# A hybrid encoder layer on one core: the gates' first weight loads, the turning of the keys, and four pins on VectorE's order

## The chip, the core and the metric

The kernel runs on one core of a Trainium2 chip. Five instruction streams work side by side: TensorE (PE, with its weight loads shown apart as PEld), VectorE (DVE), ScalarE (ACT), GpSimd (POOL) and SyncE (SP), which in this kernel only issues transfers. Each stream takes its instructions in the order in which the program lists them, so one that has to wait also holds up those behind it on its engine. Transfers are issued by SP and POOL (a few at the start by ACT) and carried by 16 DMA engines. The metric is the device time of one execution in microseconds; the time before is 641.28 us, the median of three runs (641.11 to 642.57).

## What is computed

One transformer-like layer on x of 512 tokens by 2048 features, all in float32:

```
h    = rms_norm(x, norm_w)
proj = h @ w_in                      # 2048 x 4608
q, k, v, g_attn, xr, g_lru = split(proj)
attn = softmax(rope(rms(q)) @ rope(rms(k)).T / sqrt(128)) @ v     # 8 heads, 2 key/value heads
lru  = scan_fwd(conv(xr)) + scan_bwd(conv(xr))                    # gated linear recurrence
mixed = [rms_norm(attn) * silu(g_attn), rms_norm(lru) * silu(g_lru)]
out  = x + mixed @ w_out             # 2048 x 2048
```

Every operand is held as a high part (a cast to fp32r) and a low part (the rest after subtracting the high part), and each product is three matmuls: high by high, high by low, low by high (`mm3`, lines 151 to 154).

## The kernel before

**Weights.** A weight chunk is 256 rows by 512 columns (512 KB). `wload` (line 219) issues its load on SP into one of three slots of a ring (`wring`), ACT casts its two halves to `wh` (line 216), and DVE subtracts them to `wl` (line 217), which frees the ring slot. A projection of 512 columns takes eight chunks; in each chunk PE runs 24 matmuls of 128x512, four steps of six. Loads and splits are given a priority 600 instructions ahead of their place in the text.

**Who sets the order.** PE's order is written out by hand. The order on ACT, DVE, POOL and (outside the attention) SP is chosen by a scheduler from priorities and its own estimate of when operands are ready; it is fixed when the program is built. `tc.issue_after(ins)` adds an edge of order: what the block issues on the engine of `ins` comes behind `ins` there. It adds no wait between engines. Inside the attention, SP's order is that of the text.

**The stages.** Nine projections of 512 columns follow each other on PE: two for the recurrence's input, one for keys and values, two for the queries (four heads each), then four for the gates, of which three run as `gates()` under the attention and one after it; the output projection ends the kernel. A generator `fill` yields after each of the four steps of a chunk, and `weave(fill, chain)` runs it in turn with a chain of other work: the chain yields the number of steps of `fill` to run before it goes on.

During the two query projections (64 steps) the chain is `kv` (line 581): the keys' norm and rotation, then the turning of the keys. To turn a pair of heads, `sent` (line 548) runs four DVE transposes per pair and writes the result aside to DRAM (SP, 512 KB); `landed` (line 565) reads it back with four SP transfers of 128 KB into a tile `lq`, of which there are two; `split_head` (line 575) makes the high part on ACT and the low part on DVE. The two pairs of queries from the first query projection are sent aside after its 32 steps and read back by two calls of `next_pair` (line 680). `kv` also splits the values, sums the squares of the recurrence's output (`lru_squares`), and at its end forms the factor `gbc` of the group norm.

**Gates and attention.** Before the attention, three chunks of gate weights are fetched ahead. The attention goes by units: unit `i` is head `i // 4` and block `i % 4` of 128 queries. It starts after `BEGIN` = 11 steps of the gates. `weights` (line 617) does three score matmuls into `sc`, the row maximum on DVE (`mx`, line 627), the exponential on ACT (`p`, line 629), the normalisation on POOL and a transpose on DVE (`u`, line 632). Each two units, `moved` (line 637) writes the transposed weights aside (`pd`), reads them back (`pt`), and splits them into high `ph` (ACT) and low `pl` (DVE), both on line 651; `ph` and `pl` have one buffer each, and a head has two halves. `values` (line 654) multiplies them with the values, ten units after the head's first. Two steps of the gates run between units.

A finished gate projection is evacuated by `evac_bc` (line 386): four DVE products, one for each of its four PSUM banks. This happens at units 10 and 26, which are also the units in which `values` of heads 0 and 4 are issued.

Of the kernel before, what the change touches and what calls it, by code (L numbers as in the profile page):

```python
# [21 lines left out]
NT = SEQ // P  # L22
HD = 128
NH = 8
NKV = 2
# [37 lines left out]
def hybrid_kernel(  # L63
# [20 lines left out]
    nc = tc.nc  # L84
# [63 lines left out]
    def f(ap):  # L148
        return ap.bitcast(F32)
# [42 lines left out]
    def v1(r):  # L192
        return vec[:, r : r + 1]
# [80 lines left out]
    rbc = const([P, SEQ], "rbc")  # L274
# [76 lines left out]
    def drain(fill):  # L351
        for _ in fill:
            pass
# [29 lines left out]
    hp, ap_ = [None] * (NB // 2), [None] * (NH // 2)  # L383
    sums = {}

    def evac_bc(acc):

        res = []
        with tc.high_priority():
            for a in acc:  # L390
                e = ev()
                nc.vector.tensor_mul(e, a, rbc)
                res.append(e)
        return res

# [82 lines left out]
    def lru_squares():  # L478

        hsum = pools["rot"].tile([P, 2, SEQ], F32, tag="hsum", name="hsum")  # L480
        nc.scalar.activation(hsum, hp[0], AF.Square)
        for pair in hp[1:]:
            yield 2
            sq = pools["rot"].tile([P, 2, SEQ], F32, tag="hsq", bufs=1, name=nm("hsq"))
            nc.scalar.activation(sq, pair, AF.Square)
            nc.vector.tensor_add(hsum, hsum, sq)
        sums["l"] = hsum[:, 0, :]
        nc.gpsimd.tensor_add(sums["l"], sums["l"], hsum[:, 1, :])
# [54 lines left out]
    vh = [None] * NT  # L543
    vl = [None] * NT

    asides, last_landed = [], [None]

    def sent(es, nh, *us):

        us = us or [  # L550
            pools["rot"].tile([P, NQ, 2, NT, B], F32, tag="uq", bufs=2, name=nm("uq"))
            for _ in range(nh // 2)
        ]
        for n, u in enumerate(us):
            for t, e in enumerate(es):
                nc.vector.transpose(
                    u[:, :, :, t, :].rearrange("p b h r -> p h b r"),
                    e[:, 2 * n : 2 * n + 2].rearrange("p h (b c) -> p h b c", c=B),
                )
            aside_ = dram.tile([P, NQ, 2 * SEQ // NQ], F32, name=nm("qd"), tag="qd", bufs=5)  # L560
            yield
            nc.sync.dma_start(aside_, u.rearrange("p b h t r -> p b (h t r)"))
            asides.append(aside_)

    def landed(aside_):

        to = pools["qkv"].tile([P, NQ, 2, NT, B], F32, tag="lq", bufs=2, name=nm("lq"))
        src = aside_.rearrange("(i c) b x -> b c i x", c=B)
        for b in range(NQ):
            last_landed[0] = nc.sync.dma_start(  # L570
                to[b * B : (b + 1) * B].rearrange("p i h t r -> p i (h t r)"), src[b]
            ).ins
        return to

    def split_head(pair, k, hi, lo):
# [3 lines left out]
        nc.vector.tensor_sub(lo, src, f(hi))  # L579

    def kv(es):
        drain(sent(norm_rope(es, NKV, rk), NKV))
        pair = landed(asides.pop(0))
        yield 20
        opened("wx", "right")
        for t in range(NT):
            vv = es[t][:, NKV * HD :]
            vt = aside(
                lambda *a: pools["qkv"].tile(*a, tag="v", bufs=NT, name=nm("v")), 2 * NKV * HD // H
            )  # L590
            vh[t], vl[t] = vt[:, 0, :], vt[:, 1, :]
            nc.scalar.copy(vh[t], vv)
            nc.vector.tensor_sub(vl[t], vv, f(vh[t]))
        yield from lru_squares()
        for h in range(NKV):
            yield (16, 4)[h]
            kt = pools["qkv"].tile([P, 2, SEQ], F32R, tag="kt", bufs=NKV, name=nm("kt"))
            kth[h], ktl[h] = kt[:, 0, :], kt[:, 1, :]
            split_head(pair, h, kth[h], ktl[h])
        r = group_rstd(sums["l"], "r_l", NB * P)  # L600
        yield 4
        rows(
            gbc, r,
            lambda: pools["rope"].tile([P, NT, P], F32R, tag="kv", bufs=NT, name=nm("kv")),
        )
# [6 lines left out]
        qs[h] = q[:, 0, :], q[:, 1, :]  # L612
        split_head(pairs[h // 2], h % 2, *qs[h])

    pts = {}

    def weights(q, g, t, turned_, first=()):

# [18 lines left out]
    def moved(turned_, half, his):  # L637

        aside_ = dram.tile([P, NQ, NT * H // NQ], F32, name=nm("pd"), tag="pd", bufs=2 * NH)
        nc.sync.dma_start(aside_, turned_.rearrange("p a s t c -> p a (s t c)"))  # L640
        yield
        if half == 0:
            his += [at(n, 1, (NT, 2, NQ, H // NQ), F32R) for n in ("ph", "pl")]
        pt = at("pt", 2, (NQ, NT, H // NQ))
        src = aside_.rearrange("(i r) a x -> a r i x", r=B)
        for a in range(NQ):
            nc.sync.dma_start(
                pt[a * B : (a + 1) * B].rearrange("p i s x -> p i (s x)"), src[a]
            )
        hi, lo = (v[:, :, half].rearrange("p s i x -> p i s x") for v in his[:2])  # L650
        his[2:] = [nc.scalar.copy(hi, pt).ins, nc.vector.tensor_sub(lo, pt, f(hi)).ins]  # L651
        yield

    def values(h, hi, lo):
# [25 lines left out]
    def next_pair():  # L680
        pairs.append(landed(asides.pop(0)))

    def attention():

        with tc.high_priority(AHEAD):
            for h in range(2):
                turned(h)
        yield BEGIN
        writes = []
        last, units = NH * NT, {}  # L690
        for i in range(last + NT + LATE):
            h, t = divmod(i, NT)
            if i < last:
                if t % 2 == 0:
                    u = at("u", 4, (NQ, NT, 2, B))
                first = pts[h - 2][2:] if h > 1 and t == 1 else ()
                weights(qs[h], h // G, t, u, first)
                if t == 0 and 0 < h < NH - 1:
                    turned(h + 1)
                if t % 2:  # L700
                    units[i] = moved(u, t // 2, pts.setdefault(h, []))
            for j in (i - 1, i - 3):
                if j in units:
                    next(units[j])
            if i < 2:
                es = [e[:, 2 * i : 2 * i + 2] for e in rot]
                writes.append(sent(es, 2, at("u", 4, (NQ, 2, NT, B))))
                next(writes[i])
            elif i < 4:
                drain(writes[i - 2])  # L710
            if t == 2 and h % 2 and asides:
                next_pair()
            j = i - NT - LATE
            if j >= 0 and j % NT == NT - 1:
                values(j // NT, *pts.pop(j // NT)[:2])
            yield STEPS + (last <= i < last + NT)


    def gate(gs, pairs, row, sig):

        for e, g in enumerate(gs):
            if e == 0 or sig:
                ss = [sig()] if sig else gs
                with ExitStack() as stack:
                    for parts in pts.values():
                        if parts:
                            stack.enter_context(tc.issue_after(parts[2]))
                    for s, src in zip(ss, [g] if sig else gs):
                        nc.scalar.activation(s, src, AF.Silu)
            s = ss[0] if sig else g  # L730
            yield 4
            dst = pairs[e // 2][:, e % 2, :]
            nc.vector.scalar_tensor_tensor(dst, dst, v1(row + e), s, op0=ALU.mult, op1=ALU.mult)
# [341 lines left out]
    with tc.high_priority():  # L1075
# [7 lines left out]
        first = [wsplit(raw, 0, nc.vector.tensor_copy)]  # L1083
# [4 lines left out]
    for step in proj_feat(C_XR, a1, first, given):  # L1088
# [8 lines left out]
        c, e = step  # L1097
# [30 lines left out]
    rq, rk = rope_consts()  # L1128
# [18 lines left out]
    def both():  # L1147
        yield from q_proj(C_Q, a4)
        drain(sent(rot, G))
        for _ in range(2):  # L1150
            next_pair()
        yield from q_proj(C_Q + SEQ, a5)

    fill = with_sums(both(), 3)
# [18 lines left out]
    late = []  # L1173
# [5 lines left out]
    def fetch():  # L1179
        for at_ in itertools.islice(chunks_, 1):  # L1180
            fetched.append(wload(w_in, *at_))
# [5 lines left out]
    def gates():  # L1187
        todo = iter(())
        for n, (c0, row) in enumerate(((C_GL, R_LN), (C_GL + SEQ, R_LN + 4), (C_GA, R_AN))):
            acc, wait = [], 0  # L1190
            for k, _ in enumerate(proj_feat(c0, acc, take=take)):
                if n == 0 and k >= 16 and k % 4 == 0:
                    normed(hp[k // 4 - 4])
                if wait == 0:
                    wait = next(todo, 99)
                wait -= 1
                yield
            if n < 2:
                todo = gate(evac_bc(acc), hp[2 * n : 2 * n + 2], row, None)
            else:  # L1200
                late.extend(evac_bc(acc))

    with tc.issue_after(last_landed[0]):
        for _ in range(3):
            fetch()
    fill = with_sums(gates(), 2)
    with tc.manual_schedule(engines={mybir.EngineType.SP}):
        weave(fill, attention())
# [41 lines left out]
    acc = []  # L1250
# [76 lines left out]
```

## Time and profile before

| | us |
|---|---|
| median of three runs | 641.28 |
| the profiled execution | 643.89 |
| its span, first to last instruction | 641.8 |
| PE busy | 630.6 |
| DVE busy | 492.6 |
| ACT busy | 340.7 |
| POOL busy | 102.8 |

The profiled execution is 2.6 us above the median, and 2.1 us of its time lie outside the span. PE is busy in 98% of the span; the busy time of a matmul in the profile overlaps that of the next one, so the start-to-start distance of matmuls says more than their duration. In the rows of a timeline the columns are the start, the duration, the engine, the line, the operation, what it writes and reads, its shape, and in brackets how long its engine was idle just before it and what ended that. In the view by windows each engine has its busy time and instruction count, and then follow the granted clock of TensorE, the mean busy share of the DMA engines and GB/s.

### The profile page before, as it was taken

Reading aid. Unit: us, or ns where it says so; the run is one execution under the profiler, and the core shown is the slowest. Engines: PE = TensorE matmul, PEld = TensorE weight load, DVE = VectorE, ACT = ScalarE, POOL = GpSimd, SP = SyncE. Lnnn points to the kernel's source line nnn. Section 1 sums busy time; section 2 is a strip of 40 time slices with the busy share of each in tenths; the row PEclk is TensorE's granted clock in tenths of the full one; section 3 lists DMA queues with packets and bytes.
Section 4 is the critical chain, followed back from the end, with each engine's and each line's share of the span. In section 5 each row is a group of like instructions: output and inputs, shape, how many; then the busy total and the mean of one; then the engine's idle time right before and its main releaser. Section 6 shows DMA issues by size and latency. Waiting matters only on the chain.

```text
span 641.8 us, 8300 instructions
## 1 busy us (share of the span) xinstructions
PE 630.6 (98%) x2795; PEld 517.3 (81%) x2795; DVE 492.6 (77%) x808; ACT 340.7 (53%) x582; POOL 102.8 (16%) x137
## 2 busy tenths in 40 slices
PE   9999999999999999989999999999999999999997
PEld 6888888888888788778778778888888888888885
DVE  5879688986689792777787788638979867787775
ACT  3534799479945811644484447436545544433441
POOL 0000210112002531512123211201220001010010
PEclk9999999999999999989999999999999999999999
DMA  9844585859676399369739556842996676797152
GB/s 296 286 136 134 142 199 158 180 142 199 209 230 208 103 196 248 91 173 267 214 127 270 180 176 176 241 120 65 247 241 201 200 259 216 272 358 237 66 197 99
DMA packets 71435, 124.48 MB, mean 194 GB/s; under 512 B 6376, under 2 KB 27488, under 8 KB 71392
## 3 DMA queue, kind: packets, MB, share of 16 engines
q1 hardware_dynamic: 63360, 106.11, 52.1%
q0 software_dynamic: 7712, 17.31, 14.3%
q10 hardware_dynamic: 320, 0.53, 0.3%
q8 instruction: 22, 0.36, 0.2%
q14 instruction: 21, 0.17, 0.1%
HBM read 108.72 MB, written 36.18 MB: 226 GB/s over the span
## 4 chain that ended last, share of the span: by engine, by line
PE 74%; DVE 11%; ACT 6%; DMA 4%; issue 2%; POOL 2%; SPq 0%; DVEq 0%; ACTq 0%; POOLq 0%
PE mm L948 13%; PE pj L152 13%; PE pj L153 13%; PE pj L154 13%; PE pj L948 10%; PE mm L153 3%; DVE wl L217 3%; PE mm L154 3%; PE mm L152 3%; DMA wr<-in_w_in_dram 2%; ACT wh L216 1%; ACT sh L525 1%; DVE pl L651 1%; PE mm L242 1%; DMA pt<-pd 1%
## 5 line engine op out<-in xcount | busy, mean ns | idle before, releaser
L152 PE MATMUL pj<-x,wh 128*128 128x512 f32 x376 | 148.0, 394 | 0.1
L154 PE MATMUL pj<-x,wl 128*128 128x512 f32 x376 | 147.2, 392 | 0.2 <-DVE wl L217 0.2
L153 PE MATMUL pj<-x,wh 128*128 128x512 f32 x376 | 147.2, 391 | 0.0
L216 ACT CAST wh<-wr 128x512 fp32r<-128x512 f32 x143 | 85.7, 618 | 105.6 <-PE pj L153 37.5
L217 DVE TENSOR_TENSOR wl<-wr,wh 128x512 fp32r<-128x512 f32 x144 | 99.1, 715 | 30.5 <-ACT wh L216 29.8
L800 ACT CAST wh<-wr 128x1024 fp32r<-128x1024 f32 (+1 forms) x72 | 60.7, 860 | 75.0 <-PE mm L948 37.5
L801 DVE TENSOR_TENSOR wl<-wr,wh 128x1024 fp32r<-128x1024 f32 (+1 forms) x72 | 68.7, 984 | 27.3 <-ACT wh L800 27.2
L154 PEld LDWEIGHTS pj<-x,wl 128*128 128x128 f32 x376 | 70.9, 189 | 15.6 <-DVE wl L217 0.6
L152 PEld LDWEIGHTS pj<-x,wh 128*128 128x128 f32 x376 | 70.9, 189 | 15.5 <-ACT ev L513 0.8
L153 PEld LDWEIGHTS pj<-x,wh 128*128 128x128 f32 x376 | 70.9, 189 | 14.9 <-DVE x L245 0.3
L152 PE MATMUL pj<-wh,x 128*128 128x512 f32 x192 | 75.0, 391 | 0.2 <-ACT ev L513 0.2
L154 PE MATMUL pj<-wh,x 128*128 128x512 f32 x192 | 74.7, 389 | 0.0
L153 PE MATMUL pj<-wl,x 128*128 128x512 f32 x192 | 74.7, 389 | 0.0
L824 POOL DMA_DIRECT2D t<-in_w_out_dram x40 | 33.6, 918 | 139.1 <-DMA t<-in_w_out_dram 96.7
L948 PE MATMUL mm<-wh,mh 128*128 128x512 f32 x128 | 49.8, 389 | 0.0
L948 PE MATMUL mm<-wl,mh 128*128 128x512 f32 x128 | 49.8, 389 | 0.0
L948 PE MATMUL mm<-wh,ml 128*128 128x512 f32 x128 | 49.8, 389 | 0.0
L152 PEld LDWEIGHTS pj<-wh,x 128*128 128x128 f32 x192 | 36.0, 188 | 8.3 <-ACT ev L513 0.8
L154 PEld LDWEIGHTS pj<-wh,x 128*128 128x128 f32 x192 | 36.0, 188 | 7.6
L153 PEld LDWEIGHTS pj<-wl,x 128*128 128x128 f32 x192 | 36.0, 188 | 7.3
L629 ACT ACTIVATE p<-mm,mx 128x512 f32<-128x512 f32 x32 | 21.9, 685 | 33.1 <-DVE mx L627 33.0
L631 POOL TENSOR_SCALAR p<-p,sm 128x512 f32<-128x512 f32 x32 | 23.7, 745 | 95.5 <-DVE sm L630 95.5
(203 smaller groups left out, 1050.0 us busy)
## 6 DMA issues: line engine op xcount, KB each, us to landing
wr<-in_w_in_dram SPq DMA_DIRECT2D x71, 512.0 KB, 4.2
wr<-in_w_out_dram SPq DMA_DIRECT2D x24, 512.0 KB, 5.0
t<-in_w_out_dram POOLq DMA_DIRECT2D x40, 256.0 KB, 6.9
wr<-t SPq DMA_DIRECT2D x40, 256.0 KB, 5.2
pd<-u SPq DMA_DIRECT2D x16, 512.0 KB, 3.0
pt<-pd SPq DMA_DIRECT2D x64, 128.0 KB, 3.7
t<-in_w_out_dram SPq DMA_DIRECT2D x24, 256.0 KB, 4.9
t<-t SPq DMA_DIRECT2D x16, 256.0 KB, 5.4
```

Source lines behind the costliest of these rows:

```text
L152: nc.tensor.matmul(acc, lh, rh, start=start, stop=False)
L153: nc.tensor.matmul(acc, lh, rl, start=False, stop=False)
L154: nc.tensor.matmul(acc, ll, rh, start=False, stop=stop)
L216: copy(hi, raw[:, k, :])
L217: nc.vector.tensor_sub(lo, raw[:, k, :], f(hi))
L242: nc.tensor.transpose(pt[:, t * P : (t + 1) * P], xc[:, t, ks], ident)
L629: nc.scalar.activation(p, sc, AF.Exp, bias=mx, accum_out=sm)
L631: last_pool[0] = nc.gpsimd.tensor_scalar(p, p, sm, 0.0, op0=ALU.mult, op1=ALU.add).ins
L800: nc.scalar.copy(hi[:, to], b)
L801: nc.vector.tensor_sub(lo[:, to], b, f(hi[:, to]))
L824: nc.gpsimd.dma_start(dst, src, accum_op=ALU.add)
L948: nc.tensor.matmul(dst[s], lh[:, ts_], rh, start=i == 0 and j == 0, stop=i == 7 and j == 2)
```

## The change

It has three parts.

1. The three gate chunks that are fetched ahead are no longer pinned behind the last read of the turned queries. The two calls of `next_pair`, which read the first query pairs back, move from the middle of the query projections (after the first pairs are sent) to behind these three fetches.
2. In `kv` the keys are still normed and rotated first, but their transposes and their write aside come after `lru_squares` and two more steps, the read back six steps after that, and the first split twelve steps later. The splits fall at steps 46 and 50 instead of 42 and 46; the group norm's factor follows four steps later too.
3. `moved` keeps the instructions of both halves (`his +=`), where before the second half's replaced the first's. The maximum and exponential of a head's block 0 are pinned behind the split of half 0 of the head two before, and those of block 1 behind half 1's, as before. When `values` is issued, the four split instructions of its head are kept in `summed`; the second to fourth products of a gate's evacuation are pinned behind them.

```
-    def evac_bc(acc):
+    def evac_bc(acc, first=()):
...
-            for a in acc:
+            for n, a in enumerate(acc):
                 e = ev()
-                nc.vector.tensor_mul(e, a, rbc)
+                with ExitStack() as stack:
+                    for ins in first if n else ():
+                        stack.enter_context(tc.issue_after(ins))
+                    nc.vector.tensor_mul(e, a, rbc)
...
     def kv(es):
-        drain(sent(norm_rope(es, NKV, rk), NKV))
-        pair = landed(asides.pop(0))
+        turned_k = sent(norm_rope(es, NKV, rk), NKV)
         yield 20
...
         yield from lru_squares()
+        yield 2
+        drain(turned_k)
+        yield 6
+        pair = landed(asides.pop(0))
         for h in range(NKV):
-            yield (16, 4)[h]
+            yield (12, 4)[h]
...
-        his[2:] = [nc.scalar.copy(hi, pt).ins, nc.vector.tensor_sub(lo, pt, f(hi)).ins]
+        his += [nc.scalar.copy(hi, pt).ins, nc.vector.tensor_sub(lo, pt, f(hi)).ins]
...
-                first = pts[h - 2][2:] if h > 1 and t == 1 else ()
+                first = pts[h - 2][2 + 2 * t : 4 + 2 * t] if h > 1 and t < 2 else ()
...
-                values(j // NT, *pts.pop(j // NT)[:2])
+                hi, lo, *summed[:] = pts.pop(j // NT)
+                values(j // NT, hi, lo)
...
-                            stack.enter_context(tc.issue_after(parts[2]))
+                            stack.enter_context(tc.issue_after(parts[-2]))
...
         drain(sent(rot, G))
-        for _ in range(2):
-            next_pair()
         yield from q_proj(C_Q + SEQ, a5)
...
+            evacs = evac_bc(acc, summed)
             if n < 2:
-                todo = gate(evac_bc(acc), hp[2 * n : 2 * n + 2], row, None)
+                todo = gate(evacs, hp[2 * n : 2 * n + 2], row, None)
             else:
-                late.extend(evac_bc(acc))
-
-    with tc.issue_after(last_landed[0]):
-        for _ in range(3):
-            fetch()
+                late.extend(evacs)
+
+    for _ in range(3):
+        fetch()
+    for _ in range(2):
+        next_pair()
```

The variable `last_landed` goes away with the pin. No instruction that computes is added or removed.

More of the change, by code (lines that the diff above doesn't have):

```diff
@@ L544, in hybrid_kernel @@
     vl = [None] * NT
-    asides, last_landed = [], [None]
+    asides = []
     def sent(es, nh, *us):
@@ L569, in landed @@
         for b in range(NQ):
-            last_landed[0] = nc.sync.dma_start(
+            nc.sync.dma_start(
                 to[b * B : (b + 1) * B].rearrange("p i h t r -> p i (h t r)"), src[b]
-            ).ins
+            )
         return to
@@ L613, in turned @@
         split_head(pairs[h // 2], h % 2, *qs[h])
-    pts = {}
+    pts, summed = {}, []
     def weights(q, g, t, turned_, first=()):
```

## The prediction

> **What bounds the kernel now.** I read the page's header first, then the waits of PE, then the windows in which they fall, and last the timelines of PE, DVE, ACT and SP there.
>
> ```profile
> span 641.8 us, 8300 instructions
> PE 630.6 (98%) x2795; PEld 517.3 (81%) x2795; DVE 492.6 (77%) x808; ACT 340.7 (53%) x582; POOL 102.8 (16%) x137
> ```
>
> PE bounds the kernel, and no matmul is added or taken away. So the change can win only the places where PE does not keep its pace, and lose by making new ones. The pace is in the chain of work that ended last: twelve matmuls of 128x512 in 2.72 us, 0.227 us each.
>
> ```profile
> 484.84 2.72 PE mm L948 x12
> ```
>
> The waits of PE and two windows show where it falls behind:
>
> ```profile
> PE mm L153 <- DVE pl L651: 2.8, 4, 1.0
> PE mm L154 <- DVE q L579: 2.2, 1, 2.2
> PE pj L152 <- ACT ev L513: 0.2, 1, 0.2
> PE pj L154 <- DVE wl L217: 0.2, 1, 0.2
> ...
> 271.00:280.00 9.00, 6.80 (x23) 5.15 (x22) 5.51 (x10) 3.19 (x5) 2.35 (x3) 0.81 1.01 228
> 300.00:385.00 85.00, 82.22 (x358) 66.40 (x357) 67.10 (x112) 45.74 (x86) 18.59 (x24) 1.00 0.66 196
> ```
>
> Four waits are for the low part `pl` of softmax weights, one is for the low part of a query head, and two short ones lie at the gates' beginning. In the window 271 to 280 the granted clock is 0.81. The timeline of PE gives each its true cost, the start-to-start distance less 0.227:
>
> ```profile
> 255.42 0.39 PE L154 MATMUL pj<-wh,x 128*128 128x512 f32 x1
> 255.93 0.50 PE L152 MATMUL pj<-x,wh 128*128 128x512 f32 x1
> ...
> 262.58 0.39 PE L153 MATMUL pj<-x,wh 128*128 128x512 f32 x1
> 263.15 0.50 PE L154 MATMUL pj<-x,wl 128*128 128x512 f32 x1 [0.18 <-DVE wl L217]
> ...
> 271.90 0.39 PE L153 MATMUL mm<-kt,q 128*128 128x512 f32 x1
> 274.49 0.50 PE L154 MATMUL mm<-kt,q 128*128 128x512 f32 x1 [2.20 <-DVE q L579]
> ...
> 310.51 0.39 PE L152 MATMUL mm<-ph,v 128*128 128x512 f32 x1
> 311.90 0.50 PE L153 MATMUL mm<-pl,v 128*128 128x512 f32 x1 [1.00 <-DVE pl L651]
> ```
>
> That is 0.28, 0.34, 2.36 and 1.16 us. The last shows that a wait costs 0.16 more than its bracket says, so the four waits for `pl` cost 2.8 + 4 x 0.16 = 3.4. The low clock costs (1 - 0.81) x 9 = 1.7. In all 0.28 + 0.34 + 2.36 + 1.7 + 3.4 = 8.1 us stand to be won.
>
> **Part 1, the gates' loads.** SP, then ACT, then DVE:
>
> ```profile
> 237.44 4.01 SPq L570 DMA_DIRECT2D lq<-qd  x8
> 241.69 32.53 SPq L205 DMA_DIRECT2D wr<-in_w_in_dram  x7
> ...
> 252.54 1.14 ACT L216 CAST wh<-wr 128x512 fp32r<-128x512 f32 x2 [18.33 <-DMA wr<-in_w_in_dram]
> 255.20 0.68 ACT L513 ACTIVATE ev<-pj,rstd 128x512 f32<-128x512 f32 x1
> 266.88 1.30 ACT L216 CAST wh<-wr 128x512 fp32r<-128x512 f32 x2 [1.16 <-PE pj L153]
> 268.09 1.14 ACT L578 CAST q<-lq 128x512 fp32r<-128x512 f32 x2
> ...
> 236.06 1.28 DVE L217 TENSOR_TENSOR wl<-wr,wh 128x512 fp32r<-128x512 f32 x2
> 259.55 0.69 DVE L530 TENSOR_TENSOR ev<-ev,rr 128x512 f32<-128x512 f32 x1 [3.53 <-POOL rr L271]
> 271.93 0.69 DVE L539 TENSOR_TENSOR ev<-ev,sq 128x512 f32<-128x512 f32 x1
> 272.54 1.29 DVE L217 TENSOR_TENSOR wl<-wr,wh 128x512 fp32r<-128x512 f32 x2
> 273.75 1.29 DVE L579 TENSOR_TENSOR q<-lq,q 128x512 fp32r<-128x512 f32 x2
> ```
>
> Eight reads of queries hold SP until 241.4, and only then does the first gate chunk go out. It lands at 252.5, and ACT stood 18.3 us for it. Behind that cast in ACT's order sits the first evacuation of the second query projection (255.20). Its PSUM bank was complete three steps of six matmuls before PE's last one at 255.42, at 255.42 + 0.39 - 3 x 6 x 0.227 = 251.7, so ACT is 3.5 us late. Everything behind inherits that: the squares, the reciprocal roots on POOL (which release DVE at 259.55), the rotation on DVE (to 272.6), then a gate chunk's `wl` and the query's low part at 273.75, for which PE stands from 272.1.
>
> After the change the three loads need only ring slots. The last slot comes free with the last `wl` of the query projection (236.06 + 1.28 = 237.3), the others a chunk and two chunks (5.4 us each) earlier. So the three loads can go out between about 226.5 and 237.4 instead of from 241.7 on, and the eight reads follow. Their 4.0 us of issue stay, and they land no later than the saturated transfers of the next window end:
>
> ```profile
> 237.00:253.00 16.00, 16.00 (x72) 13.22 (x71) 5.58 (x6) 0.46 (x1) 4.09 (x5) 1.00 1.05 249
> ...
> lq<-qd SPq DMA_DIRECT2D x8, 128.0 KB, 6.4
> wr<-in_w_in_dram SPq DMA_DIRECT2D x6, 512.0 KB, 11.1
> ```
>
> The DMA share is 1.05 there, so the same bytes in another order end at the same time: three loads (1.5 MB) ahead of the reads push these back by up to 1.5 MB / 249 GB/s = 6 us. A read that began at 241 and takes 6.4 lands by 254, and its first user on ACT stands at 268.09: hidden. At 11.1 us a load the first gate chunk is there by 238 and the third by 249, ACT evacuates on time, and the chain behind it moves 3.5 us forward: rotation to 269.1, `wl`, which needs ACT's casts of 266.88 (these wait for PE and do not move, done 268.2), to 270.4, and the query's low parts to 271.1 and 271.7. PE wants the first at 272.1. So the 2.36 go, with 1.0 to spare; the 0.28 go (the evacuation is what PE waited for), and the 0.34 go because the second gate chunk's last cast no longer stands behind late squares. What is late next is this same low part, and it has 1.0 us.
>
> The clock: it is low right after the 2.6 us gap and not behind the 1.4 us gap at 310.51 (1.00 in 300 to 385). I take it to go with the gap: 1.7. Part 1 is worth 0.28 + 0.34 + 2.36 + 1.7 = 4.7 us.
>
> [...]
>
> **Part 2, the keys.** Four transposes, one write of 512 KB, four reads, two casts, two subtractions and the group norm's small operations move later by one chunk of 5.4 us or (transposes, write, first reads) by about 5.
>
> ```profile
> L556 DVE STREAM_TRANSPOSE uq<-kv x4: 434/438/441, 195.8 to 202.8; 128x256 f32<-128x256 f32 x4
> L579 DVE TENSOR_TENSOR kt<-lq,kt x2: 643/664/684, 217.8 to 231.2; 128x512 fp32r<-128x512 f32 x2
> ```
>
> On DVE 4 x 0.44 = 1.8 us leave the stretch before 203 and return behind the sums of squares; nothing waits for keys until 271, so 2 x 0.66 of splits at 231 to 237 have 34 us of cover. The second split frees the tile `lq` for the second pair of queries; it then ends at about 237, when the reads are to begin: at worst they start a microsecond later, inside their cover. On SP one write and four reads move past three or four weight loads; each issue is about 0.4 us and the loads keep their priority. On POOL the group norm's two small operations, and the accumulating transfers behind them, wait up to 5.4 us longer, for sums that the output projection (first matmuls at 484.84) takes up. I take zero; the bounds are a gain of 0.1 (the last short wait of PE on an evacuation) and a loss of 1.8, the transposes if they push a `wl` that PE waits for and nothing covers them.
>
> **Part 3, the pins.** DVE around the first wait for `pl`, then around the second, with ACT:
>
> ```profile
> 308.66 0.69 DVE L392 TENSOR_TENSOR ev<-pj,rbc 128x512 f32<-128x512 f32 x1 [0.22 <-PE pj L154]
> 310.02 0.69 DVE L392 TENSOR_TENSOR ev<-pj,rbc 128x512 f32<-128x512 f32 x1 [0.67 <-PE pj L154]
> 310.63 1.22 DVE L651 TENSOR_TENSOR pl<-pt,ph 128x1024 fp32r<-128x1024 f32 x1
> ...
> 322.98 0.69 ACT L629 ACTIVATE p<-mm,mx 128x512 f32<-128x512 f32 x1 [3.21 <-DVE mx L627]
> 323.66 1.04 ACT L651 CAST ph<-pt 128x1024 fp32r<-128x1024 f32 x1
> ...
> 327.71 1.22 DVE L651 TENSOR_TENSOR pl<-pt,ph 128x1024 fp32r<-128x1024 f32 x1
> ```
>
> At 308.66 and 310.02 DVE waits for PE to finish banks of the gate, while `pl`, which PE wants at 310.7, stands behind. With the second to fourth product pinned behind it, `pl` starts by 308.5 and ends by 309.7: the 1.16 go, and again at unit 26. The pinned products lose 1.2 us; their banks are wanted four gate steps and two units later, 4 x 6 x 0.227 + 2 x 0.7 = 6.8 us, so that hides.
>
> At 322.98 ACT has stood 3.2 us for a maximum, with `ph` of half 0 behind it. The pin on block 0 puts this cast and its `pl` ahead of that exponential and maximum; half 1, whose `pl` now ends at 328.9, then follows about 2 us earlier, and its wait is only (2.8 - 2 x 1.0) / 2 + 0.16 = 0.56. The pinned maximum comes at most one `pl` (1.2) later, and its result is used several units on. The waits of heads 1 and 3 go as well, unless a read back lands late; I leave one of them. Part 3 is worth 3.4 - 0.56 = 2.8.
>
> **The sum.** 4.7 + 0 + 2.8 = 7.5 us off the profiled 643.9 gives 636.4. That execution stands 2.6 above the median, which the same gain takes from 641.3 to 633.8. From no change a measurement here can tell 0.3%, 1.9 us: faster is below 639.4.
>
> **The rivals.**
> *Only one of the two parts pays.* DVE's order is chosen anew, and the query's low part could stay behind the rotation and a gate's `wl`; or the read back, not DVE's order, makes `pl` late. For it speaks that the margin in part 1 is 1.0 us; against it, that the rows show data ready and only order in the way. 641.3 - 2.8 - 0.6 = 637.9, or 641.3 - 4.7 = 636.6. Chance 0.14.
> *The low clock stays.* [...] Against it, one dip in the whole span and that behind the longest gap. Chance 0.08.
> *The queries come too late (slower).* The eight reads now follow the loads on SP, and SP waits in order for ring slots:
>
> ```profile
> SPq L205 <- DVE wl L217: 187.3, 39, 10.4
> ```
>
> If the reads fall behind the later gate loads as well, the query's parts come behind PE. A read needs 2 us (first four issues), 6.4 to land, 0.6 to cast and 0.7 to subtract, so reads issued after 272.1 - 9.7 = 262.4 make a stall. It eats what the rest gains (0.6 + 2.8) and ends slower than 643.2 once it exceeds 2.36 + 3.4 + 1.9 = 7.7 us, with reads issued after 270. The run of seven loads ends at 241.69 + 32.53 = 274.2: behind it the stall is 11.8 us and the time 641.3 + 11.8 - 2.36 - 3.4 = 647.3. Against it, the reads stand before the fourth load in the text. Chance 0.22, other new waits of that size included.
> *The gains are given back* in new short waits, 639.4 to 643.2: chance 0.06.
>
> **How the numbers follow.** The forecast has the remaining 0.50. Faster: 0.50 + 0.14 + 0.08 = 0.72; same 0.06; slower 0.22. Its own range is 632.8 (8.1 won, and 0.4 for the spread of the runs) to 636.1 (1.8 lost in part 2, the other short wait of 0.56 in part 3). To leave out no more than 2 in 10 the range takes in the partial cases, no change, and the slower rival's cheap end: 632.5 to 644.5.
>
> **What would show it.** Right: the first load of a gate chunk ahead of the eight reads on SP; ACT's first evacuation near 251.7; the query's low part before PE's third score matmul, and the clock 1.00 there; on DVE `pl` ahead of the second product of a gate's evacuation; no wait of PE for `pl` above 0.5. Wrong: reads of queries behind a fourth gate load, a PE gap before the first scores, or a wait of PE on `wl` between 205 and 255, where it now keeps its pace.

## The result, and the profile after

The changed kernel takes 633.86 us, the median of five runs (633.61 to 634.36), against 641.28 for the kernel before (640.89 to 643.4): a ratio of 0.9877, 95% interval 0.9859 to 0.9895. The profiled execution took 634.36 against 643.89, so 9.5 us less, where the medians differ by 7.4. That difference of 2.1 us is taken up below.

Two places of the page after: its header, and the split by engine of the chain that ended last:

```profile
span 632.2 us, 8303 instructions
PE 625.8 (99%) x2795; PEld 516.4 (82%) x2795; DVE 492.9 (78%) x808; ACT 341.6 (54%) x582; POOL 104.5 (17%) x137
...
PE 98%; DMA 1%; ACT 0%; DVE 0%; ACTq 0%; DVEq 0%; issue 0%
```

The instruction counts of the engines are those of before, and so is the work of DVE and ACT to 1 us. PE alone now carries 98% of the chain. All waits of PE that are left, and then two windows, one where the scores begin and one over 80 us of the attention:

```profile
PE mm L1071 <- POOL ones L160: 1.1, 1, 1.1
PE pj L310 <- DVE wh L216: 0.6, 1, 0.6
```

```profile
267.00:276.00 9.00, 9.00 (x41) 7.26 (x40) 7.05 (x13) 4.55 (x9) 2.35 (x3) 1.00 1.02 226
296.00:376.00 80.00, 80.00 (x352) 65.80 (x351) 64.69 (x109) 45.27 (x86) 18.62 (x23) 1.00 0.69 199
```

Both waits belong to the first 10 us of the span; from there to its end no two matmuls start more than 0.34 us apart. The waits on `pl`, on `q`, on the evacuation and on `wl` are gone, PE is busy in the whole of both windows, and the clock is 1.00 in them.

**Where the 9.5 us went.** I put the matmuls of the two profiled executions side by side, in PE's order, and took the start before less the start after. The order is the same but for the group norm's small matmuls, which come a chunk later after the change (part 2). This table is worked out from some 2,800 pairs; each row is the step by which the distance grows at one place:

| place in the trace before | gained there, us | forecast, us |
|---|---|---|
| up to 211: wait on a query evacuation | 0.45 | 0 (part 2) |
| 211 to 258, most of it at the gates' start (255 to 258) | 0.67 | 0.28 |
| 263.15, `wl` of the second gate chunk | 0.5 | 0.34 |
| 274.49, low part of a query | 2.37 | 2.36 |
| the low clock behind it | 1.61 | 1.7 |
| four waits for `pl` | 1.27 + 0.65 + 0.66 + 1.27 = 3.85 | 3.4 - 0.56 = 2.8 |

**Part 1 in the trace after.** The timeline of SP, ACT, DVE and PE at the places that the forecast named:

```profile
227.14 0.39 SPq L205 DMA_DIRECT2D wr<-in_w_in_dram  x1
...
235.83 0.38 SPq L205 DMA_DIRECT2D wr<-in_w_in_dram  x1
236.27 0.93 SPq L573 DMA_DIRECT2D lq<-qd  x2
237.30 0.40 SPq L205 DMA_DIRECT2D wr<-in_w_in_dram  x1
237.74 4.67 SPq L573 DMA_DIRECT2D lq<-qd  x5
...
251.19 0.69 ACT L516 ACTIVATE ev<-pj,rstd 128x512 f32<-128x512 f32 x1 [1.42 <-PE pj L154]
...
268.54 1.29 DVE L217 TENSOR_TENSOR wl<-wr,wh 128x512 fp32r<-128x512 f32 x2
269.75 1.29 DVE L582 TENSOR_TENSOR q<-lq,q 128x512 fp32r<-128x512 f32 x2
...
270.25 0.39 PE L153 MATMUL mm<-kt,q 128*128 128x512 f32 x1
270.49 0.50 PE L154 MATMUL mm<-kt,q 128*128 128x512 f32 x1
270.82 0.39 PE L152 MATMUL pj<-x,wh 128*128 128x512 f32 x1
```

The first gate load goes out at 227.1, the other two between the reads of queries, at 235.8 and 237.3. ACT evacuates at 251.19, and what releases it is now PE, not a load. The gate chunk's `wl` stands at 268.54 and two low parts of queries from 269.75. The first of the two takes about half of the 1.29, so it ends near 270.4, and PE takes it at 270.49, 0.24 after its last matmul. That is only just in time: the matmul lasts 0.50 instead of 0.39, as the ones behind a wait do, and the next one starts 0.33 later instead of 0.227, so about 0.1 us is still lost here. In that stretch the loads have become quicker and the reads slower, as the view of the DMA issues between 225 and 270 shows (columns: size, and the median from issue to landing):

```profile
wr<-in_w_in_dram SPq DMA_DIRECT2D x7, 512.0 KB, 7.3
...
lq<-qd SPq DMA_DIRECT2D x8, 128.0 KB, 10.4
```

A gate load lands in 7.3 instead of 11.1, a read of queries in 10.4 instead of 6.4, and nothing waits for the reads.

**Part 3.** DVE around the first half of head 0, with PE behind it:

```profile
301.49 0.68 DVE L395 TENSOR_TENSOR ev<-pj,rbc 128x512 f32<-128x512 f32 x1
...
302.71 1.18 DVE L657 TENSOR_TENSOR pl<-pt,ph 128x1024 fp32r<-128x1024 f32 x1
303.82 1.27 DVE L395 TENSOR_TENSOR ev<-pj,rbc 128x512 f32<-128x512 f32 x2
...
304.86 0.39 PE L152 MATMUL mm<-ph,v 128*128 128x512 f32 x1
305.09 0.39 PE L153 MATMUL mm<-pl,v 128*128 128x512 f32 x1
```

`pl` stands behind the first product of the evacuation and ahead of the others. It ends at 303.9, and PE uses it at 305.09, one pitch after the matmul before.

### The profile page after: what moved, and what is told of

The parts are those of the page before. It is cut to its first block, busy times and chain, and to the rows that moved or that the text cites. A ratio compares the mean times of both kernels' runs of the same rounds, so it can differ in the third digit from the quotient of the medians.

```text
span 632.2 us, 8303 instructions
## 1 busy us (share of the span) xinstructions
PE 625.8 (99%) x2795; PEld 516.4 (82%) x2795; DVE 492.9 (78%) x808; ACT 341.6 (54%) x582; POOL 104.5 (17%) x137
## 4 chain that ended last, share of the span: by engine, by line
PE 98%; DMA 1%; ACT 0%; DVE 0%; ACTq 0%; DVEq 0%; issue 0%
PE pj L152 20%; PE pj L153 20%; PE pj L154 20%; PE mm L955 14%; PE pj L955 10%; PE mm L154 3%; PE mm L152 3%; PE mm L153 3%; DMA wr<-in_w_in_dram 1%; PE mm L242 1%; PE pj L310 0%; PE mm L749 0%; PE mm L290 0%; DVE cb L986 0%; ACT wh L216 0%; ACT x L244 0%
## 5 line engine op out<-in xcount | busy, mean ns | idle before, releaser
L217 DVE TENSOR_TENSOR wl<-wr,wh 128x512 fp32r<-128x512 f32 x144 | 100.4, 723 | 22.0 <-ACT wh L216 20.9
L955 PE MATMUL pj<-wl,mh 128*128 128x512 f32 x96 | 37.4, 389 | 0.0
```

What stands on the lines that cost most here:

```text
L217: nc.vector.tensor_sub(lo, raw[:, k, :], f(hi))
L955: nc.tensor.matmul(dst[s], lh[:, ts_], rh, start=i == 0 and j == 0, stop=i == 7 and j == 2)
```

## The experiments

Theory A is the prediction's own account: the three parts pay each at its place, the low clock belongs to the gap of 2.6 us, and part 2 is worth nothing. The theories set against it stand in the expectations with their numbers. Kernels of one group ran on one chip and share its runs of the kernel before, whose median was 643.1 in the first group, 643.42 in the second and 642.46 in the third; so each time is read against its own group.

### The kernel before, once more

No edit. This asks how far its executions lie apart, and whether each has the low clock.

> The kernel before, unchanged, to see how far its executions differ from each other. [...] Rival (the dip is a fixed cost): all executions have the same clock and differ by under 1 us.

642.36 (640.03 to 644.35, 12 runs) against 643.1 (639.59 to 645.84, 28 runs); ratio 0.9991, 0.9971 to 1.0012. Over all 40 executions the mean clock sorts the times:

| mean clock of the execution | executions | median us | from - to |
|---|---|---|---|
| 0.997 and below | 16 | 644.09 | 643.04 - 645.84 |
| 0.998 | 5 | 643.13 | |
| 0.999 and above | 19 | 641.79 | 639.59 - 643.25 |

In the other two groups 5 of 7 and 2 of 12 executions of the kernel before have a mean clock of 0.997 or below. The profiled execution has a gap as long as the first one's, and no low clock in it. The timeline of ACT and DVE, and then the window:

```profile
255.41 0.62 ACT L216 CAST wh<-wr 128x512 fp32r<-128x512 f32 x1 [1.58 <-DMA wr<-in_w_in_dram]
255.93 0.68 ACT L513 ACTIVATE ev<-pj,rstd 128x512 f32<-128x512 f32 x1
...
274.49 1.28 DVE L579 TENSOR_TENSOR q<-lq,q 128x512 fp32r<-128x512 f32 x2
```

```profile
271.00:280.00 9.00, 6.80 (x30) 5.30 (x30) 7.06 (x13) 3.29 (x6) 2.35 (x3) 1.00 0.99 208
```

PE is busy 6.80 us in the window, as in the execution of the prediction, but gets 30 matmuls done instead of 23: 7 x 0.227 = 1.6 us. So the gap is in both profiled executions of this kernel, and a low clock in some 4 of 10 executions of this group. The cast at 255.41 is 0.74 later than in the first profile (254.67), yet the gap is not longer: PE has already lost time at the gates' start, to the evacuation behind that cast: the distance there is 1.38 (255.29 to 256.67), where the first profile has 0.51. A later landing is thus paid in two places, at the gates' start and at the gap. The median of before contains only part of the 1.7; the profiled execution that the sum was made from has it whole.

### Part 1 alone

The kernel before, with this edit:

```
-        for _ in range(2):
-            next_pair()
         yield from q_proj(C_Q + SEQ, a5)
...
-    with tc.issue_after(last_landed[0]):
-        for _ in range(3):
-            fetch()
+    for _ in range(3):
+        fetch()
+    for _ in range(2):
+        next_pair()
```

> The kernel before with part 1 alone (the three gate fetches unpinned, the two reads of query pairs behind them). Theory A (part 1 pays by itself: the first gate chunk lands early, ACT evacuates the query projection on time, the query's low part is ready): 641.3 - 4.7 = 636.6, no PE gap before the first scores, the four waits for pl still there. Rival B (part 1 needs the keys out of its way): a gap of over 1 us stays before the first scores, 639 or more.

638.45 (638.15 to 639.05, 9 runs); ratio 0.9935, 0.9915 to 0.9954: 4.65 us off 643.1. The timeline of ACT and DVE:

```profile
251.69 0.69 ACT L513 ACTIVATE ev<-pj,rstd 128x512 f32<-128x512 f32 x1 [1.42 <-PE pj L154]
270.25 1.29 DVE L579 TENSOR_TENSOR q<-lq,q 128x512 fp32r<-128x512 f32 x2
```

PE's waits on `q` and `wl` are gone; those on `pl` stand as they were, four with 2.8 us in all. Moving the loads takes the gap away by itself, and the spread between executions with it: 0.9 us here, 6.3 for the kernel before.

### Part 2 alone, and the change without part 1

The first is the kernel before with the edit of `kv` only:

```
-        drain(sent(norm_rope(es, NKV, rk), NKV))
-        pair = landed(asides.pop(0))
+        turned_k = sent(norm_rope(es, NKV, rk), NKV)
...
+        yield 2
+        drain(turned_k)
+        yield 6
+        pair = landed(asides.pop(0))
         for h in range(NKV):
-            yield (16, 4)[h]
+            yield (12, 4)[h]
```

> The kernel before with part 2 alone (keys transposed, sent aside and read back later). Theory A: no more than 0.5 us either way, 640.8 to 641.8, the gap of 2.6 us before the first scores and the four waits for pl unchanged. Rival B (the keys' move is what frees the stage): the gap shrinks, 638 or less.

663.74 (663.04 to 664.53); ratio 1.0321, 1.0277 to 1.0365. The second is the changed kernel with the fetches pinned again and `next_pair` back in its old place:

> The changed kernel with part 1 undone (fetches pinned behind the last read, reads in their old place). Theory A: 633.9 + 4.7 = 638.6, the gap of 2.6 us before the first scores back, no wait for pl. Rival B (the keys' move did it): 635 or less.

660.49 (659.2 to 661.03); ratio 1.0264, 1.0246 to 1.0282. Both times miss every expectation, and for one reason. The list `asides` is taken from the front. With the reads of queries in their old place and the keys sent aside later, those reads come before the keys' own: the keys are read from the aside of a query pair and a query pair from that of the keys, so the output is another, and the three reads stand in another order on the two tiles `lq`. The trace of part 2 alone, first the waits of PE and of SP's queue, then SP's timeline:

```profile
PE pj L152 <- ACT wh L216: 23.5, 1, 23.5
...
SPq L570 <- DVE q L579: 30.2, 1, 30.2
```

```profile
234.43 35.08 SPq L570 DMA_DIRECT2D lq<-qd  x8
269.55 12.18 SPq L205 DMA_DIRECT2D wr<-in_w_in_dram  x5
```

The third tile waits for a buffer that the queries' splits free, 30.2 us, and the gates' loads stand behind that read on SP; PE then waits 23.5 for the first gate chunk. This doesn't measure what part 2 is worth. It shows that part 2 needs part 1's move of the reads, and what a read with no free buffer costs on a queue that works in order.

### Part 3 alone

The kernel before with all pins; the main lines of the edit are:

```
+                    for ins in first if n else ():
+                        stack.enter_context(tc.issue_after(ins))
...
-        his[2:] = [nc.scalar.copy(hi, pt).ins, ...
+        his += [nc.scalar.copy(hi, pt).ins, ...
...
-                first = pts[h - 2][2:] if h > 1 and t == 1 else ()
+                first = pts[h - 2][2 + 2 * t : 4 + 2 * t] if h > 1 and t < 2 else ()
```

> The kernel before with part 3 alone (both pins). Theory A: the gap before the first scores stays, the four waits for pl go, 641.3 - 3.4 = 637.9 (638.5 if one is left). Rival C (pl was late because the read back was late, and the pins only relabel the wait): waits for pl of 2 us or more stay in sum, 640 or more.

640.24 (635.21 to 641.59, 10 runs); ratio 0.9944, 0.9917 to 0.997: 2.9 us off, with 1.9 to 5.3 in its interval, where 3.4 was expected. All four waits for `pl` are gone. The longest wait of PE behind the start is now this one:

```profile
PE mm L154 <- DVE q L582: 0.5, 1, 0.5
```

and the timeline of ACT and DVE is:

```profile
251.74 0.62 ACT L216 CAST wh<-wr 128x512 fp32r<-128x512 f32 x1 [1.22 <-DMA wr<-in_w_in_dram]
252.26 0.69 ACT L516 ACTIVATE ev<-pj,rstd 128x512 f32<-128x512 f32 x1
270.81 1.28 DVE L582 TENSOR_TENSOR q<-lq,q 128x512 fp32r<-128x512 f32 x2
```

The wait on `q` is 0.5 here, not 2.2. This is the fastest of the ten executions, 635.21, and its third half of gate weights landed in time for a cast at 251.74, where the profiled executions of the unedited kernel had it at 254.67 and 255.41. The first evacuation follows that cast in ACT's order, and the low part of the query follows the evacuation at a nearly constant distance in all traces: 18.55 here, 18.55 and 18.56 in the two of before, 18.56 in part 1 alone, 18.56 after. So the gap's size hangs on when that load lands (and, where the load is so late that PE stands at the gates' start, on how much is paid there first), and differs from one execution to the next.

### The change without part 2

The changed kernel with `kv` as before.

> The changed kernel with part 2 undone (keys turned early again). Theory A: within 0.5 us of the changed kernel's 633.9, at most one short wait of 0.4 us back at the start of the second query projection. Rival B: the gap before the first scores comes back in part, 635 or more.

634.95 (634.51 to 635.55); ratio 0.987, 0.9852 to 0.9887 against 643.42. One wait of PE is back:

```profile
PE pj L152 <- ACT ev L516: 0.2, 1, 0.2
```

In the timeline this is a distance of 0.59 between matmuls at 209.78 and 210.37, 0.36 above the pitch, and the next one, to 210.71, is 0.11 above it. The times can't tell 0.5 us across groups, so part 2 is worth the 0.47 that this trace shows, or the 0.45 of the two profiled executions: little, but not the zero of the sum. The wait stands in all five traces without part 2 and in none of the nine with it. The rows show how it goes: the evacuation stands on ACT behind squares of the recurrence's output, which wait for a sum on DVE. Before, that sum starts at 204.62, behind the keys' transposes, and the evacuation at 209.71; after, they start at 202.43 and 208.40.

### The change without the pin on the evacuation

```
...
-                    for ins in first if n else ():
-                        stack.enter_context(tc.issue_after(ins))
```

> The changed kernel without the pin on the gates' evacuations, the pin on block 0's maxima kept. Theory A (two causes, two pins): the waits of heads 0 and 4 come back, 1.2 us each, those of heads 1 and 3 do not: 633.9 + 2.4 = 636.3. Rival D (one chain: the late evacuation is what makes head 1 late too): three waits or more, 636.8.

636.61 (636.12 to 636.75); ratio 0.9894, 0.988 to 0.9909; 1.7 above the kernel without part 2 of the same group (the changed kernel itself was not run in this group; with part 2's 0.47 taken off that kernel, the pin is worth about 2.1). PE's wait, and the timeline of DVE at the first of two places:

```profile
PE mm L153 <- DVE pl L654: 2.0, 2, 1.0
```

```profile
303.80 0.69 DVE L392 TENSOR_TENSOR ev<-pj,rbc 128x512 f32<-128x512 f32 x1 [0.67 <-PE pj L154]
304.41 1.22 DVE L654 TENSOR_TENSOR pl<-pt,ph 128x1024 fp32r<-128x1024 f32 x1
```

This is the picture of before, six us earlier: DVE waits for PE's banks with `pl` behind. The waits of heads 0 and 4 are back, each a distance of 1.39 on PE, and those of heads 1 and 3 are not. The pin does what the prediction said, for these two heads alone.

### The change without the pin on block 0

```
-                first = pts[h - 2][2 + 2 * t : 4 + 2 * t] if h > 1 and t < 2 else ()
+                first = pts[h - 2][4:6] if h > 1 and t == 1 else ()
```

> The changed kernel without the pin on block 0's maxima, the pin on the gates' evacuations kept. Theory A: the waits of heads 1 and 3 come back, 0.6 us each, 633.9 + 1.2 = 635.1. Rival D: only head 3's comes back, 634.5, since head 1 was late by the evacuation. Rival E (the pin on maxima is idle): 633.9.

635.68 (635.49 to 635.84); ratio 0.9881, 0.9866 to 0.9896. The wait of PE:

```profile
PE mm L153 <- DVE pl L657: 0.8, 2, 0.4
```

The waits of heads 1 and 3 are back, each a distance of 0.79 on PE (322.20 - 321.41 and 355.74 - 354.95), 0.56 above the pitch. The time is 0.7 above the kernel without part 2, so by the same reckoning this pin is worth about 1.2. The two pins divide the four waits between them.

### The changed kernel again, beside the next three

> The changed kernel, unchanged, beside the next three on the same chip. It has no PE gap in the middle stages, so its executions should lie within 1 us of each other (theory A: the spread of the kernel before comes from its gaps).

634.25 (634.18 to 634.82) against 642.46; ratio 0.9865, 0.9845 to 0.9884. Its four executions lie within 0.64 us. The two medians of the changed kernel, here and in the first measurement, are 0.4 us apart.

### The reads first, then the loads

The changed kernel with SP's order put back and nothing else changed: both pairs of queries are read, and only then do the three loads go out.

```
...
-    for _ in range(3):
-        fetch()
     for _ in range(2):
         next_pair()
+    before_it = last_landed[0]
+    for _ in range(3):
+        with tc.issue_after(before_it):
+            fetch()
+        before_it = loads_done[nc.sync]
```

> The changed kernel with the three gate loads issued behind the eight reads of the queries, everything else as in the changed kernel: part 1 undone in SP's order alone, and with the keys' aside read first, as it must be. Theory A: the gap of over 2 us before the first scores and the wait at the gates' beginning come back, in part of the executions with the low clock: 4.7 us over the changed kernel, 3 us at least. Rival B (it is the keys' later turning that makes room): no gap over 1 us, within 1 us of the changed kernel.

637.4 (636.44 to 638.65); ratio 0.9913, 0.9889 to 0.9936; 3.15 above the changed kernel of its group. The timeline of SP, ACT, DVE and PE, and then the window:

```profile
234.37 6.01 SPq L573 DMA_DIRECT2D lq<-qd  x8
240.48 2.41 SPq L205 DMA_DIRECT2D wr<-in_w_in_dram  x3
...
252.73 0.62 ACT L216 CAST wh<-wr 128x512 fp32r<-128x512 f32 x1 [2.63 <-DMA wr<-in_w_in_dram]
253.26 0.68 ACT L516 ACTIVATE ev<-pj,rstd 128x512 f32<-128x512 f32 x1
...
271.81 1.28 DVE L582 TENSOR_TENSOR q<-lq,q 128x512 fp32r<-128x512 f32 x2
...
272.55 0.64 PE L154 MATMUL mm<-kt,q 128*128 128x512 f32 x1 [2.21 <-DVE q L582]
```

```profile
271.00:280.00 9.00, 7.45 (x26) 5.99 (x27) 5.53 (x11) 3.96 (x7) 2.35 (x3) 0.81 0.90 182
```

The evacuation is 2.07 later than after the change and the query's low part 2.06: the whole chain of part 1, moved by one cause. The low clock is back in this execution and, by the mean clocks, in one other of the four. Theory A had asked for 4.7, and at least 3; the two short waits at the gates' start have not come back, with the third cast 1.9 us earlier than the 254.67 of before. From that evacuation to the query's low part, ACT and DVE run the same instructions in the same order before, after and here. Ahead of it the order on DVE differs a little: the gates' first `wl` stands ahead of the group norm's products after the change, among them here and behind them before.

### Attention begun one and two steps earlier

To measure how much room the query's low part has, `BEGIN` is 10 and then 9 instead of 11: PE asks for the low part one or two gate steps (6 x 0.227 = 1.36 each) sooner.

> The changed kernel with the attention begun one gate step earlier (10 instead of 11), so that PE wants the query's low part 1.36 us earlier. Theory as predicted (1.0 us to spare): a gap of 0.4 us. Theory A2 (the trace after: the low part ends at 270.43 and PE takes it at 270.49, nothing to spare, because PE itself came earlier): a gap of 1.3 us before the first scores and 1.4 us more time. No low clock by either.

635.58 (635.34 to 636.07), 1.33 above the changed kernel, and every execution at clock 1.0:

```profile
268.81 0.39 PE L153 MATMUL mm<-kt,q 128*128 128x512 f32 x1
270.39 0.50 PE L154 MATMUL mm<-kt,q 128*128 128x512 f32 x1 [1.19 <-DVE q L582]
```

The step is lost almost whole: 1.58 - 0.227 = 1.35. With 1.0 us to spare it would have cost 0.4. There is no room.

> The changed kernel with the attention begun two gate steps earlier (9), so that PE wants the low part 2.7 us earlier. Theory A (a gap of about 2.6 us brings the low clock in part of the executions): a gap of 2.7 us, 2.8 us more time, and in half of the executions a mean clock of 0.997 or less and 1.7 us more. [...]

646.68 (645.21 to 647.62, 9 runs); ratio 1.0061, 1.004 to 1.0081: 12.4 above the changed kernel of its group, where 4.5 at most was expected. The wait for the query is as expected; what comes with it isn't. The new wait of PE, and in the timeline the gap and DVE at unit 10:

```profile
PE mm L153 <- DVE pl L657: 6.1, 6, 1.4
```

```profile
267.45 0.39 PE L153 MATMUL mm<-kt,q 128*128 128x512 f32 x1
270.38 0.50 PE L154 MATMUL mm<-kt,q 128*128 128x512 f32 x1 [2.54 <-DVE q L582]
...
304.27 0.69 DVE L395 TENSOR_TENSOR ev<-pj,rbc 128x512 f32<-128x512 f32 x1 [0.19 <-PE pj L154]
304.88 1.22 DVE L657 TENSOR_TENSOR pl<-pt,ph 128x1024 fp32r<-128x1024 f32 x1
```

Unit 10 now comes two gate steps before the gate's last matmul, so even the first product of the evacuation, which has no pin, waits for its bank with `pl` behind it. Five more waits for `pl` follow in later heads, and the six make up most of the excess: on PE's timeline they cost 8.4 us, and the one for the query 2.8; that they stem from this first one I read from late writes aside and reads back, and no run tests it. Six of the nine executions had a mean clock of 0.997 or less (median 646.9), three had more (645.4), the profiled one among them.

## Why the prediction was right

**The bound and the places** were right: PE keeps its pace everywhere now, and the gains lie at the places quoted, each taken away by the part that was named for it (part 1 alone 4.65, part 3 alone 2.9, together 7.5 within one group; the change in the third group 8.2, 7.5 to 10.0 by its interval).

**Part 1's chain** was right from SP to PE, and SP's old order alone brings the late chain back. Two of its details were not. The loads do not all go out ahead of the reads. Only the first waits for a ring slot; the second stands on SP behind the first read, and that read waits 5.3 us, to 235.4, for the queries' write aside to land. And the load that decides is not the first, as the step had it, but the second, because in ACT's order the evacuation stands behind the cast of its first half too. Both left the result as it was, since the transfers that lost, the reads, had over 13 us of cover: the last goes out at 242.1 and lands at 252.3, and ACT casts the first of them at 266.4.

**The margin of 1.0 us** is the step that failed. The step put the low parts at 271.1 and 271.7 and PE at 272.1. The first low part ends 0.7 earlier than that, but PE comes 1.6 earlier, because the short waits ahead are gone (0.45 + 0.67 + 0.5), and it takes the part within 0.1 of its end: its weight load stands 0.27 for it, though the view of PE's waits shows nothing. Beginning the attention one step earlier cost 1.35 of 1.36. So the rival in which the query's low part stays late was closer than its 0.14 said: a stall of about 0.1 us has begun, and any further lateness adds to it in full.

**The clock** went with the gap, as the step took it. None of the nine executions of the changed kernel (five in the first measurement, four in the third group) has a mean clock of 0.997 or below, and none of the nine of part 1 alone; the kernel with the reads first has the dip back, 0.81 in the window; the shorter gap of 1.19 us idle never brought it. What the step missed is that the dip follows the gap only at times. Mean clocks of 0.997 or below stand in 16 of 40 executions of before, 6 of 10 with part 3 alone, 2 of 4 with the reads first, 6 of 9 with the attention two steps earlier.

The trace of before shows what a dip costs. From 275.99 to 279.40 the granted clock is 0.50 there, and matmuls start 0.43 apart instead of 0.227:

```profile
276.00 0.63 PE L154 MATMUL pj<-x,wl 128*128 128x512 f32 x1
276.42 0.63 PE L152 MATMUL pj<-x,wh 128*128 128x512 f32 x1
...
279.41 0.40 PE L153 MATMUL mm<-kt,q 128*128 128x512 f32 x1
```

These are eight distances in 3.41 us, so 3.41 - 8 x 0.227 = 1.6 us are lost, the 1.61 of the alignment. In five profiled executions PE idles over 1 us for the query's low part; the table has that time, from the view of its waits or its timeline, beside the clock in the window 271 to 280:

| trace | PE idle in the gap, us | clock in the window |
|---|---|---|
| attention two steps earlier | 2.54 | 1.00 |
| the kernel with the reads first | 2.21 | 0.81 |
| before | 2.20 | 0.81 |
| before, once more | 2.2 | 1.00 |
| attention one step earlier | 1.19 | 1.00 |

The longest of these gaps has no dip behind it, and of the three of 2.2 us two have one and the third has none. So the length of the gap does not settle it, and what else does is not shown. The rival in which the low clock stays is refuted by the changed kernel, which has no such gap and a clock of 1.00 in the window 267 to 276.

**Part 2** was taken as zero with a gain of 0.1 at most; it gained 0.45 to 0.47. The wait is the one that its bound named; the row of the waits gave 0.2 for it, and I didn't read its distance on PE's timeline, as I had done for the others. The cover was larger than the step needed: the keys' second split ends at 230.9 in the trace after, not near 237.

**Part 3** was put at 2.8 and gave 3.85 in the alignment. I left one wait of 0.56 standing for a late read back, and none stayed; the rest is that a wait of PE costs more than the 0.16 added to the bracket. The distance behind the restart is too long as well, by 0.11: at the first wait for `pl`, PE goes on from 311.90 to 312.24, which is 0.34 instead of 0.227. Four times 0.11 is 0.44, and the same 0.11 is missing in the terms for the gates' start and for `wl`.

**The median.** The sum of 7.5 was made against the profiled execution, where the gain was 9.5, and then taken off the median, where it was 7.4. Two errors of 2 us lie in opposite directions: the terms were too small by 0.45 + 0.4 + 0.2 + 1.05 - 0.1, and the profiled execution stood 2.6 above the median, most of it the low clock (1.6), which a median of before holds only in part. The step "the same gain takes from 641.3 to 633.8" is wrong as reasoning; that it lands within 0.1 us of the measured 633.86 is luck, since the two errors cancel. The executions of before show the size of the second: 644.09 with the low clock, 641.79 without.

No kernel that was run is faster than the changed one.

## What to carry to other kernels

Look for the transfer that an in-order engine waits for, even where that engine is idle half of the time: ACT's wait for one gate load set, 18.6 us later, when PE got its query. The executions of this kernel spread by 6 us (639.6 to 645.8), and by less than 1 once its wait for a transfer was gone (part 1 alone); so where executions spread, read a wait's size in more than one of them before subtracting it from a median. And when a stall is removed, reckon the next margin against the consumer's new time, not the old one: PE came 1.6 us earlier and used up the room. To price a wait of PE, read two distances on its timeline: that of the matmul that waits and the next one.

## What was unexpected in the hardware

The low clock came behind a gap in which PE idled 2.2 us, and not each time: of two gaps of 2.6 us in the same kernel, one window of 9 us had 0.81 and the other 1.00. What parted them is not shown.

A wait of PE cost 0.27 us more than the idle time that the profile shows: in 34 of the 37 waits between 195 and 480 us in ten traces, 0.16 in its own distance and 0.11 in the next, for waits of 0.1 to 2.5 us. In the trace of before, the wait of 2.20 us has a distance of 2.59 and one of 0.34 behind it, the wait of 0.38 has 0.77 and 0.34.

The order of issue on SP moves the landing of transfers by 3 to 5 us: in the kernel with the reads first, whose edit touches nothing but that order, the DMA issues between 225 and 270 are

```profile
wr<-in_w_in_dram SPq DMA_DIRECT2D x6, 512.0 KB, 11.3
...
lq<-qd SPq DMA_DIRECT2D x8, 128.0 KB, 5.3
```

against 7.9 and 9.8 in the changed kernel of the same group (medians, with three or four later loads among them). What was issued earlier came quicker, at the cost of what stood behind; the runs don't show why.
